# Gate projection of a decoder layer by seven block products

## The chip, the cores and the metric

The kernel runs on one NeuronCore of a Trainium2 chip, in one launch. The metric is the device time of that launch in microseconds (us); lower is better. The engines are TensorE (PE, matrix products), VectorE (DVE), ScalarE (ACT), GpSimd (POOL) and SyncE (SP, which here only issues DMAs). Each engine has its own queue of instructions.

## The reference

One decoder layer on 512 tokens of 1024 channels, all in float32: a mixer (pooling and block-sparse attention), a gated MLP with a causal convolution, and at the end an embedding that is gated by a projection of x. The change concerns the last line.

```python
y = jnp.concatenate([y_pool, y_attn], axis=-1) @ w_out[i]
x = x + rms_norm(y, g_mix_post[i])
h = rms_norm(x, g_ffn_pre[i])
x = x + rms_norm(conv_ffn(h, w_up[i], conv_w[i], conv_b[i], w_down[i]), g_ffn_post[i])
x = x + (p[i] @ w_ple[i]) * jax.nn.sigmoid(x @ w_ple_gate[i])
```

Here x is (512, 1024), `w_ple_gate` (1024, 1024), p (512, 256) and `w_ple` (256, 1024). The MLP has 2816 hidden channels.

## The kernel before

All products keep float32 accuracy by a split: each operand is written as a high and a low part in a reduced format, and three matmuls (low x high, high x low, high x high) are summed in PSUM. `mm3` (lines 190 to 194) issues the three, `split` (lines 196 to 198) makes the parts: ACT copies the high part, DVE subtracts it from the source.

Weights go through the class `_Weights`. Chunks of 1 MB are loaded by SP into one of 2 `raw` buffers and split into pairs (`wh`, `wl`), 6 of which can exist. `take` hands out the next pair; `ahead(n)` issues the splits for n pairs beyond those taken, and with the last split of a chunk the load of the chunk two further on. Nothing reorders this: the order of the Python calls is the order on each engine.

The stages: input projection, attention and pooling (to about 150 us of the profile's clock), output projection and second norm (to about 205), up projection (`project`, 44 column blocks of 24 matmuls; convolution and GELU in `gate_post`, `gelu`, `value_post`), the down projection, and the end. The down projection computes its 2x2 block product with seven products in place of eight (`GROUPS`). Four of these need differences of weight blocks: during the up stage POOL loads rows of `w_down`, forms them in `weight_sums` (line 679) and writes them to the DRAM tile `tsum`, from where they are loaded and split like other weights.

The end starts at about 540 us. `embedding` computes p @ w_ple for four token tiles (48 matmuls, eight outputs). `third_norm` finishes the norm of the MLP and adds the residual x; for tiles 2 and 3 this lies between the embeddings. `put_transposed` transposes x on PE (eight 128x128 blocks a tile) and splits the result into `xT`. `gate_part` is the gate projection: for each column half and token tile a sum over 8 blocks of 128 channels, 24 matmuls. The last output is done in two parts of 256 columns. `gate_out` (lines 789 to 795) finishes an output: sigmoid on ACT, multiplication by the embedding and addition of x on DVE, store on SP. Splits of gate weights stand between the outputs, by `W.ahead((0, 1, 2, 4)[t])`.

Of the kernel before, what the change touches and what calls it, by code (L numbers as in the profile page):

```python
# [24 lines left out]
P = 128  # L25
S = 512
# [34 lines left out]

class _Weights:
# [22 lines left out]

    def load(self, between=None):
        c = self.loaded
        srcs, axis = self.chunks[c]
        raw = self.pool.tile([P, 2048], F32, tag="raw", name=f"raw{c}", bufs=self.RAW)
        if axis == 0:  # L90
            self.raw[c] = raw.rearrange("p (s a b) -> p s a b", s=2, a=2)
            for s, src in enumerate(srcs):
                self.nc.sync.dma_start(self.raw[c][:, s, :src.shape[1], :], src)
        else:
            src = srcs[0]
            self.raw[c] = raw.rearrange("p (a b) -> p a b", a=src.shape[1])
            n = 2 if c < 2 else 1
            step = src.shape[1] // n
            for i in range(n):
                part = slice(i * step, (i + 1) * step)  # L100
                self.nc.sync.dma_start(self.raw[c][:, part, :], src[:, part, :])
                if between is not None:
                    between(i)
        self.loaded += 1

    def ahead(self, n):

        while self.split < min(self.used + n, 2 * len(self.chunks)):
# [3 lines left out]
            raw, (srcs, axis) = self.raw[c], self.chunks[c]  # L112
            if axis == 0:
                view = raw[:, s, :srcs[s].shape[1], :]
            else:
                half = raw.shape[axis] // 2
                part = slice(s * half, (s + 1) * half)
                view = raw[:, part, :] if axis == 1 else raw[:, :, part]
# [5 lines left out]
            self.nc.scalar.copy(pair[0], view)  # L124
            self.nc.vector.tensor_sub(pair[1], view, pair[0].bitcast(F32))  # L125
            self.pairs[self.split] = pair
            self.split += 1
            if s == 1:
                del self.raw[c]
                while self.loaded < min(c + 1 + self.RAW, len(self.chunks)):  # L130
                    self.load()
# [8 lines left out]
def hybrid_layer(ctx, tc, x, p, rel_bias, g_mix_pre, g_mix_post, g_ffn_pre, g_ffn_post, w_in, w_pool,  # L140
# [45 lines left out]
    for n in range(2):  # L186
        for k0 in (0, 4):
            W.rows(w_ple_gate, k0, 4, 512 * n, 512)
# [445 lines left out]
    def value_post(f, pv):  # L634
        dve.scalar_tensor_tensor(M[:, f, :], c_.pop(f), 0.5, pv, op0=ALU.mult, op1=ALU.mult)
        if f >= NK:
            token_sums(f)
# [4 lines left out]
    M = lp.tile([P, NF, S], F32, name="M")  # L642
# [3 lines left out]
    def tokens01(f, n=1):  # L646
        return M[:, f:f + n, :2 * P]

    def tokens23(f, n=1):
        return M[:, f:f + n, 2 * P:]  # L650
# [10 lines left out]
    tw = tw_ctx.enter_context(tc.tile_pool(name="tw", bufs=2, reuse_waits="tile"))  # L661
# [3 lines left out]
    def weight_load():  # L665
        k = len(b_)
        if k < NK:
            b = tw.tile([P, 4, 512], F32, tag="b", name=f"b{k}")
            for i, row in enumerate((k, NK + k)):
                src = w_down[row * P:(row + 1) * P, :].rearrange("p (n c) -> p n c", n=2)  # L670
# [3 lines left out]
    def weight_sums(k):  # L674

        weight_load()
        b = b_[k]
        for o, i0, i1 in ((1, 1, 0), (3, 3, 1), (0, 3, 0), (2, 2, 3)):
            pool.tensor_tensor(out=b[:, o, :], in0=b[:, i0, :], in1=b[:, i1, :], op=ALU.subtract)  # L679
        pool.dma_start(tsum[:, k, :, :], b)  # L680
# [30 lines left out]
    for fb in range(1, NF // 2):  # L711
        for post in (gate_post, value_post):
            for f in (2 * fb, 2 * fb + 1):
# [3 lines left out]
                if u % 2 == 0 and u // 2 < NK:  # L717
                    weight_sums(u // 2)
                u += 1
                if u == 36:  # L720
# [30 lines left out]
    for g, (i, ks) in enumerate(GROUPS):  # L751
# [7 lines left out]
        if ks[-1] == NK - 1:  # L759
            for a in range(2):  # L760
# [7 lines left out]
                elif i == 6:  # L768
# [4 lines left out]
                    if a:  # L773
                        todo = steps([third_norm(t, M[:, 2 * t:2 * t + 2, :]) for t in range(2)])
# [11 lines left out]
    E = M[:, :2 * NT, :].rearrange("p (t n) q -> p t (n q)", n=2)  # L786
    turn = iter(range(2 * NT, 18))

    def gate_out(t, c0, width, ps):
        cols = slice(c0, c0 + width)  # L790
        sg = M[:, next(turn), :width]
        act.activation(sg, ps, AF.Sigmoid)
# [6 lines left out]
    tags = iter(("mm", "mm", "s") * 4)  # L799
# [8 lines left out]
    def gate_part(t, n, c, width):  # L808
        ps = bank(f"g{t}_{n}_{c}")
        sub = [[q[:, :, c:c + width] for q in w] for w in wq]  # L810
        token_product(ps[:, c:c + width], t, sub, range(KD), True, True, h_stationary)
        gate_out(t, n * 512 + c, width, ps[:, c:c + width])

    todo = third_norm(2, M[:, 18:20, :])
    for t in range(NT):
        for n in range(2):
            embedding(t, n)
            next(todo, None)
        if t < 2:
            put_transposed(t, X[t], "pt" if t else "s")  # L820
        if t == 1:
            W.ahead(2)
            todo = third_norm(3, M[:, 20:22, :])
    put_transposed(2, X[2], "pt")
    wq = [W.take() for _ in range(4)]
    for t in range(NT):
        gate_part(t, 0, 0, 512)
        if t == 0:
            put_transposed(3, X[3], "s")
        W.ahead((0, 1, 2, 4)[t])  # L830
    wq = [W.take() for _ in range(4)]
    for t in range(NT - 1):
        gate_part(t, 1, 0, 512)
    for c in range(0, 512, 256):
        gate_part(NT - 1, 1, c, 256)
# [41 lines left out]
```

## Time and profile before

| what | us |
|---|---|
| median of 3 runs (lowest, highest) | 606.15 (604.91, 606.17) |
| the profiled execution | 605.64 |
| its span, first to last instruction | 603.7 |
| PE busy in the span | 596.4 |
| DVE, ACT, POOL busy | 388.4, 280.0, 181.8 |

A profile is one execution, on its own clock that starts at the first instruction. Successive matmuls overlap in it: one of 512 columns is shown with 0.39 us, and the next starts 0.23 us after it. What a matmul costs is therefore read from the distance of starts. A "releaser" is the instruction whose end set a waiting one free.

### The profile page before, as it was taken

The numbers are of one execution on the slowest core, as the hardware profiler recorded it, in microseconds if no ns is written. First come the engines' busy times: TensorE is split into PE (matmuls) and PEld (weight loads), VectorE is DVE, ScalarE is ACT, GpSimd is POOL, SyncE is SP. The second block draws the span as 40 slices with busy tenths as digits, with TensorE's granted clock in tenths as the row PEclk, the third lists the DMA queues.
The fourth block names the chain that finished last, engine by engine and source line by source line (L and its number), as shares of the span: only waits on it lengthen the run. The fifth ranks groups of instructions, "written<-read, shape, count | busy, mean of one in ns | idle before, by whom it ended". The sixth has DMA issues, their size and how long they took to land.

```text
span 603.7 us, 7410 instructions
## 1 busy us (share of the span) xinstructions
PE 596.4 (99%) x2832; PEld 495.9 (82%) x2832; DVE 388.4 (64%) x538; ACT 280.0 (46%) x457; POOL 181.8 (30%) x198
## 2 busy tenths in 40 slices
PE   9999999999999999999999999999999999999997
PEld 5888888888888988888888888888888788888876
DVE  4643676877478657655755764654778776788432
ACT  5532665665455433423532433342555666657320
POOL 2300230046324446666555784214310000002000
PEclk9999999999999999999999999999999999999999
DMA  8675203023660686776757734233174677661211
GB/s 290 209 278 192 70 2 114 25 71 106 209 209 0 243 316 215 283 268 231 259 206 286 270 141 140 71 85 124 69 244 157 202 251 248 210 211 63 105 54 52
DMA packets 56491, 102.35 MB, mean 170 GB/s; under 512 B 2963, under 2 KB 32495, under 8 KB 55048
## 3 DMA queue, kind: packets, MB, share of 16 engines
q1 hardware_dynamic: 48344, 67.71, 34.1%
q0 software_dynamic: 8112, 34.17, 14.8%
q8 instruction: 22, 0.36, 0.3%
q14 instruction: 13, 0.11, 0.1%
HBM read 86.12 MB, written 18.37 MB: 173 GB/s over the span
## 4 chain that ended last, share of the span: by engine, by line
PE 94%; DVE 3%; ACT 1%; issue 1%; POOL 0%; DVEq 0%; POOLq 0%
PE gate L192 6%; PE gate L193 6%; PE valu L192 6%; PE valu L193 6%; PE valu L194 6%; PE gate L194 6%; PE d L192 6%; PE d L194 5%; PE d L193 5%; PE g L193 2%; PE g L194 2%; PE y L193 2%; PE y L192 2%; PE y L194 2%; PE g L192 2%; PE tr L233 2%
## 5 line engine op out<-in xcount | busy, mean ns | idle before, releaser
L125 DVE TENSOR_TENSOR wl<-raw,wh 128x1024 fp32r<-128x1024 f32 (+1 forms) x120 | 149.0, 1249 | 25.4 <-ACT wh L124 24.8
L124 ACT CAST wh<-raw 128x1024 fp32r<-128x1024 f32 (+1 forms) x120 | 120.5, 1021 | 25.5 <-DMA raw<-in_w_down 8.8
L679 POOL TENSOR_TENSOR b<-b 128x512 f32<-128x512 f32 x44 | 69.0, 1577 | 11.2 <-DMA b<-in_w_down 9.4
L192 PE MATMUL gate<-hT,wl 128*128 128x512 f32 x160 | 62.3, 389 | 0.0
L193 PE MATMUL gate<-hT,wh 128*128 128x512 f32 x160 | 62.3, 389 | 0.0
L194 PE MATMUL gate<-hT,wh 128*128 128x512 f32 x160 | 62.2, 389 | 0.0
L192 PE MATMUL valu<-hT,wl 128*128 128x512 f32 x160 | 62.2, 389 | 0.0
L193 PE MATMUL valu<-hT,wh 128*128 128x512 f32 x160 | 62.2, 389 | 0.0
L194 PE MATMUL valu<-hT,wh 128*128 128x512 f32 x160 | 62.2, 389 | 0.0
L192 PE MATMUL d<-wh,ml 128*128 128x512 f32 x154 | 60.0, 390 | 0.7 <-DVE ml L198 0.7
L193 PE MATMUL d<-wl,mh 128*128 128x512 f32 x154 | 59.9, 389 | 0.0
L194 PE MATMUL d<-wh,mh 128*128 128x512 f32 x154 | 59.9, 389 | 0.0
L619 ACT ACTIVATE c<-gate,cols 128x512 f32<-128x512 f32 x20 | 15.5, 776 | 81.4 <-PE gate L194 81.4
L620 DVE SCALAR_TENSOR_TENSOR c<-gate,cols,c 128x511 f32<-128x511 f32 x20 | 14.9, 747 | 43.5 <-ACT c L619 43.5
L464 POOL TENSOR_TENSOR u<-u 128x512 f32<-128x512 f32 x10 | 11.6, 1156 | 81.0 <-ACT u L460 80.6
L194 PEld LDWEIGHTS gate<-hT,wh 128*128 128x128 f32 x160 | 30.0, 188 | 6.3
L194 PEld LDWEIGHTS valu<-hT,wh 128*128 128x128 f32 x160 | 30.0, 188 | 6.3
L192 PEld LDWEIGHTS valu<-hT,wl 128*128 128x128 f32 x160 | 30.0, 188 | 6.3
L222 POOL TENSOR_SCALAR rd<-msd 128x1 f32<-128x1 f32 x4 | 3.1, 783 | 106.4 <-ACT M L217 106.4
L192 PEld LDWEIGHTS gate<-hT,wl 128*128 128x128 f32 x160 | 30.0, 188 | 6.2
L193 PEld LDWEIGHTS valu<-hT,wh 128*128 128x128 f32 x160 | 30.0, 188 | 6.1
L193 PEld LDWEIGHTS gate<-hT,wh 128*128 128x128 f32 x160 | 30.0, 188 | 6.1
(205 smaller groups left out, 1309.9 us busy)
## 6 DMA issues: line engine op xcount, KB each, us to landing
raw<-in_w_up SPq DMA_DIRECT2D x22, 1024.0 KB, 5.3
b<-in_w_down POOLq DMA_DIRECT2D x22, 512.0 KB, 5.0
tsum<-b POOLq DMA_DIRECT2D x11, 1024.0 KB, 5.0
raw<-tsum SPq DMA_DIRECT2D x20, 512.0 KB, 5.0
raw<-in_w_down SPq DMA_DIRECT2D x15, 512.0 KB, 5.9
raw<-in_w_in SPq DMA_DIRECT2D x6, 1024.0 KB, 6.7
raw<-in_w_out SPq DMA_DIRECT2D x4, 1024.0 KB, 5.1
raw<-in_w_ple_gate SPq DMA_DIRECT2D x4, 1024.0 KB, 5.3
```

The costliest lines, as they stand in the source:

```text
L124: self.nc.scalar.copy(pair[0], view)
L125: self.nc.vector.tensor_sub(pair[1], view, pair[0].bitcast(F32))
L192: pe.matmul(o, st[1], mv[0], start=first, stop=False, skip_group_check=more)
L193: pe.matmul(o, st[0], mv[1], start=False, stop=False, skip_group_check=more)
L194: pe.matmul(o, st[0], mv[0], start=False, stop=last, skip_group_check=more)
L222: pool.tensor_scalar(r, ms, add, None, op0=ALU.add)
L233: pe.transpose(ps[:, k * P:(k + 1) * P], src[:, (4 * c + k) * P:(4 * c + k + 1) * P], ident)
L464: pool.tensor_tensor(out=nxt[:, 16:], in0=src[:, 16:], in1=src[:, 16 - (1 << lvl):16 + S - (1 << lvl)], op=ALU.add)
L619: act.activation(c0, pg, AF.Identity, bias=cw[:, 3, f:f + 1], scale=cw[:, 2, f:f + 1])
L620: dve.scalar_tensor_tensor(c0[:, 1:], pg[:, :S - 1], cw[:, 1, f:f + 1], c0[:, 1:], op0=ALU.mult, op1=ALU.add)
L679: pool.tensor_tensor(out=b[:, o, :], in0=b[:, i0, :], in1=b[:, i1, :], op=ALU.subtract)
```

## The change

The gate projection, too, is now computed from seven block products. x is cut into token halves (tiles 0, 1 and 2, 3) and channel halves, `w_ple_gate` into four blocks of 512x512. A product is 12 matmuls x 2 token tiles, all of 512 columns. Products 1, 2 and 3 take blocks of the weight as they are; 4, 5, 6 and 7 take differences of blocks.

Those differences are made in the up stage. After the 11 rounds for `w_down`, `weight_sums` runs four more, on `w_ple_gate`; `split_sums`, called one and two up products after the next round's begin, splits a block in ACT and DVE, and SP writes its high and low parts to the DRAM tile `gsum`. The pool `tw` has 3 buffers for loaded rows in place of 2, and one buffer each for the high and low part; it is closed one up product later. At the end the pairs of products 5, 6, 7 and 4 come from `gsum` straight into the `wh` and `wl` buffers, with no split (`pairs_of`).

On the side of x, the first half (tiles 0 and 1) is transposed and split as before, and POOL adds the two parts up again (`unsplit`) to have them in one piece. For the second half one sum is made from PSUM on DVE, the other differences on POOL (`sums`), and each is split before the product that needs it (`split_sum`). Partial results are copied from PSUM (`keep_sum`) and added on DVE (`add_sum`); outputs of 512 columns are finished by `gate_out`, the last one too. The order at the end is: embeddings and transposes of tiles 0 and 1, product 1, the third norms and embeddings of tiles 2 and 3, their transposes, then products 2, 5, 6, 3, 7, 4. `M` is now two tiles; the second one's place is used again for `S24`.

The core of the diff:

```diff
+    def split_sums(k, half):
+
+        part = slice(2 * half, 2 * half + 2)
+        pair = [tw.tile([P, 2, 512], F32R, tag=f"b{c}", name=f"b{c}{k}_{half}", bufs=1) for c in "hl"]
+        split(pair, b_[k][:, part, :])
+        for c in range(2):
+            dst = gsum[part, :, c, k - NK, :].rearrange("b p c -> p b c")
+            sp.dma_start(dst, pair[c].bitcast(F32))
...
-                if u % 2 == 0 and u // 2 < NK:
-                    weight_sums(u // 2)
+                if u < 2 * NK:
+                    if u % 2 == 0:
+                        weight_sums(u // 2)
+                else:
+                    k, step = divmod(u - 2 * NK, 3)
+                    if step and 0 < k <= KG:
+                        split_sums(NK + k - 1, step - 1)
+                    elif step == 0:
+                        weight_sums(NK + k)
...
+    def unsplit(a):
+        for c, raw in enumerate((A11, A12)):
+            hi, lo = (q[:, a, KG * c:KG * (c + 1)].bitcast(F32) for q in hT)
+            pool.tensor_tensor(out=by_tiles(raw[a]), in0=hi, in1=lo, op=ALU.add)
+
+    def second_half(a):
+
+        t = 2 + a
+        ps = x_transposed(t, 0, "s")
+        act.copy(A21[a], ps)
+        ps = x_transposed(t, 1, "s" if a else "pt")
+        split([q[:, t, KG:] for q in hT], by_tiles(ps))
+        dve.tensor_add(A22[a], ps, A21[a])
+
+    def sums():
+
+        for a in range(2):
+            pool.tensor_tensor(out=A21[a], in0=A11[a], in1=A21[a], op=ALU.subtract)
+            pool.tensor_tensor(out=A11[a], in0=A22[a], in1=A11[a], op=ALU.subtract)
+        for a in range(2):
+            pool.tensor_tensor(out=A12[a], in0=A12[a], in1=A11[a], op=ALU.subtract)
+        for a in range(2):
+            split([q[:, 2 + a, :KG] for q in hT], by_tiles(A22[a]))
...
+    def product(i, a):
+        for k in range(KG):
+            mm3(acc[i][a], operand(i, a, k), [q[:, k % 2, :] for q in wq[k // 2]],
+                k == 0 and i in (1, 2, 5), k == KG - 1, i not in (1, 2, 5))
...
+    for t in range(2, NT):
+        for n in range(2):
+            embedding(t, n)
+        keep_sum(1, t - 2)
+    W.ahead(4)
+    for a in range(2):
+        second_half(a)
+    sums()
+    wq = [W.take() for _ in range(2)]
+    W.ahead(4)
+    acc[2] = [bank(f"g2_{a}") for a in range(2)]
+    for a in range(2):
+        product(2, a)
+        add_sum(1, 2, a)
+        split_sum(6, a)
+    for a in range(2):
+        gate_out(a, 0, rows_of(held[1], a), rows_of(held[1], a))
+    wq = [W.take() for _ in range(2)]
+    W.ahead(4)
+    acc[5] = acc[3] = [bank(f"g5_{a}", "s") for a in range(2)]
+    for a in range(2):
+        product(5, a)
+        keep_sum(5, a)
+        split_sum(3, a)
...
+    for a in range(2):
+        product(7, a)
+        add_sum(5, 7, a)
+    wq = [W.take() for _ in range(2)]
+    product(4, 0)
+    for a in range(2):
+        gate_out(2 + a, 1, rows_of(held[5], a), rows_of(held[5], a))
+    gate_out(2, 0, acc[4][0], rows_of(held[4], 0))
+    product(4, 1)
+    gate_out(3, 0, acc[4][1], rows_of(held[4], 1))
```

Where instructions stand now. First ACT, around the last embedding copies (`M<-e`). Before (`xT0` is the high part of the transposes, `wh114` and `wh115` that of the third and fourth pair of gate weights; L792 is the sigmoid):

```order
L806 COPY M_1936<-e2_1_4603 128x512
L806 COPY M_1936<-e3_0_4612 128x512
L806 COPY M_1936<-e3_1_4621 128x512
L197 CAST xT0_4521<-tr2_0_4629 128x512
L197 CAST xT0_4521<-tr2_1_4636 128x512
L124 CAST wh114_4643<-raw57_4478 128x1024
L124 CAST wh115_4647<-raw57_4478 128x1024
L792 ACT_TABLE_LOAD
L792 ACTIVATE M_1936<-g0_0_0_4653 128x512
```

and now, from the row behind the copy of the last embedding `e3_1` on (`g1_1` is the second of product 1's banks, `wh114` and `wh115` product 2's weights, `z2` and `z3` the room for sums of x, `S24` operands of product 6, L853 the sigmoid):

```order
L933 COPY M0_1937<-g1_1_4666 128x512
L143 CAST wh114_4738<-raw57_4556 128x1024
L143 CAST wh115_4742<-raw57_4556 128x1024
L895 COPY z2_3693<-tr2_0_4756 128x512
L225 CAST xT0_4598<-tr2_1_4762 128x512
L895 COPY z3_3694<-tr3_0_4770 128x512
L225 CAST xT0_4598<-tr3_1_4776 128x512
L225 CAST xT0_4598<-z2_3693 128x512
L225 CAST xT0_4598<-z3_3694 128x512
L225 CAST S24_4597<-z0_3691 128x512
L225 CAST S24_4597<-z1_3692 128x512
L853 ACT_TABLE_LOAD
```

The casts of `wh114` and `wh115` stood behind the embedding copies and two transposes' casts; now they stand behind the copies of the last embedding and of a bank of product 1 and ahead of the transposes, and the sigmoid table is loaded after the casts of product 6's operands.

Second DVE, from the casts' low halves on. Before, outputs (L793, L794) alternate with splits:

```order
L125 TENSOR_TENSOR wl114_4644<-raw57_4478,wh114_4643 128x1024
L125 TENSOR_TENSOR wl115_4648<-raw57_4478,wh115_4647 128x1024
L793 TENSOR_TENSOR M_1936<-M_1936 128x512
L794 TENSOR_TENSOR M_1936<-M_1936,S1_1937 128x512
L198 TENSOR_TENSOR xT1_4522<-tr3_0_4682,xT0_4521 128x512
L198 TENSOR_TENSOR xT1_4522<-tr3_1_4689,xT0_4521 128x512
L793 TENSOR_TENSOR M_1936<-M_1936 128x512
L794 TENSOR_TENSOR M_1936<-M_1936,S1_1937 128x512
L125 TENSOR_TENSOR wl116_4726<-raw58_4512,wh116_4725 128x1024
```

and now (`g2_0`, `g2_1` are product 2's banks, `wl120` and `wl121` product 3's weights, the last row product 3's first operand):

```order
L226 TENSOR_TENSOR xT1_4599<-z3_3694,xT0_4598 128x512
L937 TENSOR_TENSOR M0_1937<-M0_1937,g2_0_4802 128x512
L226 TENSOR_TENSOR S24_4597<-z0_3691,S24_4597 128x512
L937 TENSOR_TENSOR M0_1937<-M0_1937,g2_1_4803 128x512
L226 TENSOR_TENSOR S24_4597<-z1_3692,S24_4597 128x512
L854 TENSOR_TENSOR M0_1937<-M0_1937 128x512
L855 TENSOR_TENSOR M0_1937<-M0_1937,S1_1939 128x512
L854 TENSOR_TENSOR M0_1937<-M0_1937 128x512
L855 TENSOR_TENSOR M0_1937<-M0_1937,S1_1939 128x512
L144 TENSOR_TENSOR wl120_4843<-raw60_4754,wh120_4842 128x1024
L144 TENSOR_TENSOR wl121_4847<-raw60_4754,wh121_4846 128x1024
L226 TENSOR_TENSOR S24_4597<-z0_3691,S24_4597 128x512
```

In front of product 3's weights and operand there now stand the splits for product 6 and the two finished outputs.

Third SP, the DMAs of the end. Before:

```order
L101 DMA raw56_4441<-in_w_ple_gate 128x4x512
L101 DMA raw57_4478<-in_w_ple_gate 128x4x512
L101 DMA raw58_4512<-in_w_ple_gate 128x4x512
L101 DMA raw59_4651<-in_w_ple_gate 128x4x512
L795 DMA out<-M_1936 128x512 x7
L795 DMA out<-M_1936 128x256 x2
```

and now (pairs 116 and 117 belong to product 5, 118 and 119 to 6, 122 and 123 to 7, 124 and 125 to 4):

```order
L141 DMA wh118_4794<-gsum_75 128x1024
L141 DMA wl118_4795<-gsum_75 128x1024
L141 DMA wh119_4798<-gsum_75 128x1024
L141 DMA wl119_4799<-gsum_75 128x1024
L856 DMA out<-M0_1937 128x512 x2
L141 DMA wh122_4884<-gsum_75 128x1024
L141 DMA wl122_4885<-gsum_75 128x1024
L141 DMA wh123_4888<-gsum_75 128x1024
L141 DMA wl123_4889<-gsum_75 128x1024
L141 DMA wh124_4926<-gsum_75 128x1024
```

The loads of products 7 and 4 now stand behind the first two stores of outputs.

## Rows read from the trace of the kernel before

**Rows 1.** Page: busy time of each engine, and GB/s in 40 slices.

```profile
PE 596.4 (99%) x2832; PEld 495.9 (82%) x2832; DVE 388.4 (64%) x538; ACT 280.0 (46%) x457; POOL 181.8 (30%) x198
...
GB/s 290 209 278 192 70 2 114 25 71 106 209 209 0 243 316 215 283 268 231 259 206 286 270 141 140 71 85 124 69 244 157 202 251 248 210 211 63 105 54 52
```

**Rows 2.** Timeline, PE at the end: start, duration (us), line, operation.

```profile
589.67 0.39 PE L194 MATMUL g<-wh,xT 128*128 128x512 f32 x1
...
593.07 0.39 PE L194 MATMUL g<-wh,xT 128*128 128x512 f32 x1
593.29 0.28 PE L192 MATMUL g<-wh,xT 128*128 128x256 f32 x1
...
598.93 0.28 PE L194 MATMUL g<-wh,xT 128*128 128x256 f32 x1
```

**Rows 3.** Timeline, PE, two gaps of the gate projection.

```profile
556.09 0.39 PE L192 MATMUL g<-wh,xT 128*128 128x512 f32 x1
556.50 0.50 PE L193 MATMUL g<-wl,xT 128*128 128x512 f32 x1
...
579.06 0.39 PE L192 MATMUL g<-wh,xT 128*128 128x512 f32 x1
579.78 0.50 PE L193 MATMUL g<-wl,xT 128*128 128x512 f32 x1 [0.33 <-DVE wl L125]
```

**Rows 4.** Timeline, DVE: last addition of a 512- and of a 256-column output.

```profile
594.85 0.69 DVE L794 TENSOR_TENSOR M<-M,S 128x512 f32<-128x512 f32 x1
...
600.12 0.43 DVE L794 TENSOR_TENSOR M<-M,S 128x256 f32<-128x256 f32 x1
```

**Rows 5.** DMA issues, stores at 595.6 and 600.6: KB, us to landing.

```profile
out<-M SPq DMA_DIRECT2D x1, 256.0 KB, 2.0
...
out<-M SPq DMA_DIRECT2D x1, 128.0 KB, 1.9
```

**Rows 6.** Timeline, PE: last embedding matmul, first gate matmul.

```profile
552.25 0.39 PE L194 MATMUL e<-wh,pT 128*128 128x512 f32 x1
...
553.28 0.48 PE L192 MATMUL g<-wh,xT 128*128 128x512 f32 x1
```

**Rows 7.** Timeline, ACT, from the last embedding on.

```profile
552.68 0.58 ACT L806 COPY M<-e 128x512 f32<-128x512 f32 x1 [0.78 <-PE e L194]
...
554.12 2.02 ACT L124 CAST wh<-raw 128x1024 fp32r<-128x1024 f32 x2
556.16 1.28 ACT L792 ACT_TABLE_LOAD   x1
559.33 0.60 ACT L792 ACTIVATE M<-g 128x512 f32<-128x512 f32 x1 [1.89 <-PE g L194]
```

**Rows 8.** Timeline, DVE: norm of the last tile, two weight splits.

```profile
552.24 1.28 DVE L738 SCALAR_TENSOR_TENSOR S<-z,rd,S 128x1024 f32<-128x1024 f32 x1 [0.75 <-POOL rd L223]
...
555.22 2.36 DVE L125 TENSOR_TENSOR wl<-raw,wh 128x1024 fp32r<-128x1024 f32 x2
```

**Rows 9.** Groups of DVE, 215 to 353 us: count, busy, mean ns, idle before.

```profile
L125 DVE TENSOR_TENSOR wl<-raw,wh 128x1024 fp32r<-128x1024 f32 x24 | 34.8, 1451 | 4.1 <-ACT wh L124 4.1
L630 DVE SCALAR_TENSOR_TENSOR sq<-sq,c 128x512 f32<-128x512 f32 x14 | 16.3, 1165 | 0.8 <-ACT sq L629 0.8
...
L635 DVE SCALAR_TENSOR_TENSOR M<-c,valu 128x512 f32<-128x512 f32 x12 | 8.2, 682 | 8.8 <-PE valu L194 8.8
```

**Rows 10.** The same, 360 to 428 us.

```profile
L125 DVE TENSOR_TENSOR wl<-raw,wh 128x1024 fp32r<-128x1024 f32 x13 | 15.8, 1217 | 0.0
...
L630 DVE SCALAR_TENSOR_TENSOR sq<-sq,c 128x512 f32<-128x512 f32 x7 | 4.8, 683 | 0.0
```

**Rows 11.** Line 679 on POOL: ns minimum/median/maximum, first and last start.

```profile
L679 POOL TENSOR_TENSOR b<-b x44: 1275/1310/2280, 213.7 to 352.1; 128x512 f32<-128x512 f32 x44
```

**Rows 12.** Windows: busy us (count) PE, PEld, DVE, ACT, POOL, PEclk, DMA share, GB/s.

```profile
208.00:224.00 16.00, 16.00 (x107) 14.69 (x106) 9.65 (x11) 6.33 (x9) 6.02 (x5) 1.00 1.02 379
360.00:400.00 40.00, 40.00 (x178) 33.15 (x177) 21.00 (x26) 13.35 (x17) 12.79 (x13) 1.00 0.33 106
```

More of the change, by code (lines that the diff above doesn't have):

```diff
@@ L185, in hybrid_layer, with gate_sum @@
     W.rows(w_ple, 0, 2, 0, D)
-    for n in range(2):
-        for k0 in (0, 4):
-            W.rows(w_ple_gate, k0, 4, 512 * n, 512)
+    gsum = dram.tile([4, P, 2, KG, 512], F32, name="gsum")
+    def gate_sum(i):
+        place = {7: 0, 5: 1, 4: 2, 6: 3}[i]
+        return [[gsum[place, :, c, k0:k0 + 2, :] for c in range(2)] for k0 in (0, 2)]
+    for i in GATE:
+        if i in (1, 2, 3):
+            row, n = {1: (0, 0), 2: (KG, 0), 3: (KG, 1)}[i]
+            W.rows(w_ple_gate, row, KG, 512 * n, 512)
+        else:
+            W.pairs_of(*gate_sum(i))
     def mm3(o, st, mv, first, last, more=False):
@@ L666, in weight_load @@
         k = len(b_)
[L667 to L670, printed above, removed]
+        if k < NK + KG:
+            w, k, half = (w_down, k, NK) if k < NK else (w_ple_gate, k - NK, KG)
+            b = tw.tile([P, 4, 512], F32, tag="b", name=f"b{len(b_)}")
+            for i, row in enumerate((k, half + k)):
+                src = w[row * P:(row + 1) * P, :].rearrange("p (n c) -> p n c", n=2)
                 pool.dma_start(b[:, 2 * i:2 * i + 2, :], src)
@@ L773, in hybrid_layer @@
                     if a:
[L774 removed]
+                        todo = steps([third_norm(t, M(2 * t, 2)) for t in range(2)])
         W.ahead(4)
@@ L816, in hybrid_layer @@
         for n in range(2):
             embedding(t, n)
[L818 to L835, printed above, removed]
+        first_half(t)
+    next(thirds[0])
+    wq = [W.take() for _ in range(2)]
+    acc[1] = acc[6] = acc[7] = acc[4] = [bank(f"g1_{a}", "pt") for a in range(2)]
+    for a in range(2):
+        product(1, a)
+    next(thirds[1])
+    for _ in steps(thirds):
+        pass
+    for a in range(2):
+        unsplit(a)
+    for t in range(2, NT):
+        for n in range(2):
+            embedding(t, n)
+        keep_sum(1, t - 2)
@@ new lines, in hybrid_layer @@
+    wq = [W.take() for _ in range(2)]
+    W.ahead(4)
+    for a in range(2):
+        product(6, a)
+        keep_sum(6, a)
+        split_sum(7, a)
+    wq = [W.take() for _ in range(2)]
+    W.ahead(4)
+    for a in range(2):
+        product(3, a)
+        gate_out(a, 1, add_sum(6, 3, a), rows_of(held[6], a))
+    wq = [W.take() for _ in range(2)]
+    W.ahead(4)
+    for a in range(2):
+        product(7, a)
+        add_sum(5, 7, a)
+    wq = [W.take() for _ in range(2)]
+    product(4, 0)
```

114 lines of the change are left out of this document (82 added, 32 removed).

## The prediction

> **What bounds the kernel now.** First I read busy shares and the chain that ended last: TensorE (PE) is busy for 596.4 of 603.7 us [rows 1], so a matmul less is time less, as long as nothing takes its place. Then the PE timeline of the gate projection. Its 512-column matmuls start 0.2267 us apart (15 between 589.67 and 593.07), the 256-column ones at the end 0.12 us apart (47 between 593.29 and 598.93) [rows 2]. At two places the gap is longer, 0.41 us at 556.50 and 0.72 us at 579.78, the second waiting for a weight split on VectorE (DVE); with the slow restart of 0.34 us after each, some 0.9 us is lost [rows 3]. Then the end: from the start of the last matmul to the end of the last add 1.62 us with 256 columns, and 2.47 us for an earlier output with 512 [rows 2, 4]; the stores land 1.9 and 2.0 us after issue [rows 5].
>
> **What goes.** Before, the gate projection is 4 row tiles x 2 column halves x 8 blocks x 3 terms, 168 matmuls of 512 columns and 48 of 256 (the last output is cut in two). Now it is 7 products x 2 tiles x 4 blocks x 3 terms, 168 of 512. What goes is the 48 x 0.12 = 5.76 us. The two waits of 0.9 us go too, since the splits behind which PE waited stand elsewhere. Embeddings (48 matmuls) and 32 transposes stay.
>
> **What comes late instead.** I follow the new order on the old clock; up to 540 us nothing in this part moves. Product 1 (24 matmuls, 5.44 us) is put ahead of the embeddings of tiles 2 and 3, so that their last matmul starts at 552.25 + 5.44 = 557.69 [rows 6]. Sixteen transposes later (eight took 0.8 us between 552.25 + 0.23 and 553.28 [rows 6]; I allow 0.85) PE is ready for product 2 at 559.6. Its weights are cast only now: ScalarE (ACT) has to copy the last embedding (0.43 us after its last matmul started, as at 552.68) and the held product first, each a step of 0.5 us, so the cast runs from 559.1 to 560.15 [rows 6, 7]. DVE's half takes 1.22 us [rows 10], to 561.4 at best. PE's second matmul was due at 559.85: 1.55 us lost.
>
> It is rather more, for GpSimd now works in this stretch. Rows show what that does to DVE. While GpSimd (POOL) forms the weight sums of the down projection, a DVE operation with both inputs in SBUF takes 1451 ns (128x1024) or 1165 ns (128x512), one with an input in PSUM 682 ns [rows 9]; with POOL mostly idle the first two take 1217 and 683 ns [rows 10]. So an operation with two SBUF inputs and a POOL operation exclude each other. POOL's own 128x512 subtraction takes 1310 ns in the median and up to 2280, one DVE operation more [rows 11]. The four additions that rebuild the transposes stand behind the norms of tiles 2 and 3: their mean squares come on ACT at 547.9 and 549.0 by the same stepping, then DVE's two operations per tile (the longer 1.28 [rows 8]) alternate with POOL's small ones until 554.2. The first addition (1.31), DVE's last norm operation (1.28) and three more additions take it to 560.7; the weight split starts then and ends at 562.0. I take 2.1 us lost.
>
> The Trainium skill has this as a lock (SBUF — State Buffer, Terms): GpSimd and VectorE arbitrate for one shared port pair, held for the whole instruction, and the loser blocks fully. The rows agree for two SBUF inputs and not for a PSUM input. Read literally it makes a rival, below.
>
> Products 2, 5 and 6 then run without a gap, to 567.2, 572.65 and 578.1. Product 3 is the next that I see late. Behind the second weight split (563.1) DVE splits one transposed half and adds the next, 0.6 each, to 564.3; POOL's differences start there. The fourth is product 6's second operand, and three DVE splits with SBUF inputs get in between: 564.3 + 4 x 1.31 + 3 x 0.68 = 571.6. ACT casts it (0.62), loads the sigmoid table (1.28) and makes the first sigmoid (0.60) [rows 7], to 574.0. DVE meanwhile waits for POOL's fifth difference, splits (to 573.5), and waits for the sixth, to 574.85. Then stand in DVE's queue, in this order, four multiplies and adds of the first two outputs (2.7 us), the two weight splits of product 3 (2.36 us) [rows 8] and its operand's low half (0.6): 580.45. PE was ready at 578.1: 2.35 us lost. Behind it products 3, 7 and 4 follow without a gap: product 7's operands are split by 582.3, and PE comes to them at 585.9.
>
> Of the table load the Trainium skill says (ScalarE: Activation LUTs, What ACT_TABLE_LOAD costs) that a drain of about 1.38 us comes on top of 1.28 us. In this trace ACT waits for PE after the load until 559.33 [rows 7], so no run here shows it. By it the end would be some 0.6 us later, 604.8 (an estimate from that page).
>
> **The end.** The last output now has 512 columns: 2.47 - 1.62 = +0.85 us, its store +0.1 us; and the last matmul starts 0.2267 instead of 0.12 us before PE's end, -0.11.
>
> **Cost nothing, and why.** Sixteen more POOL subtractions (21 us and more) and eight more splits (10 to 12 us of DVE, 8 of ACT) fall between 342 and 420 us. There POOL, DVE and ACT are busy 12.8, 21.0 and 13.4 of 40 us [rows 12], and an up product has four others, 21.8 us, before its PSUM bank is used again. SP gets 16 stores of 512 KB that wait for those splits, ahead of the loads of w_up and w_down; these are issued two chunks, four products, ahead, so a few us late is early enough. DMA is at 106 GB/s there; 12.6 MB more is about 33 us at the 379 GB/s that it holds for 16 us elsewhere [rows 12], in some 75. The single buffer of each half makes the second split wait for the first store to land; a store of 256 KB lands 2.0 us after issue [rows 5], one of 512 KB by that rate some 0.7 us later, and the splits are 5.44 us apart. If that cover failed, a product would wait for what is missing, 1 to 4 us. Below nothing: I see no edit before 540 us that takes work off PE. Tiles 2 and 3 are normed under product 1 and the embeddings (11 us) and are done at 556.8, two us ahead of their transposes. A stall of 2 us is longer than any the trace has; that PE keeps its full clock through it (granted 1.00, the 2.4 GHz level) [rows 12] is assumed.
>
> **Sum.** -5.76 - 0.9 + 2.1 + 2.35 + 0.85 + 0.1 - 0.11 = -1.4 us against the profiled execution of 605.64 us (span 603.7 and 1.9 around it): 604.2. The timed runs of before have their median 0.5 us higher, at 606.15, so against them the gain may read 1.9 us, and 0.2% (about what a measurement of this kernel can tell from no change) is 1.2 us.
>
> **Rivals.**
> A, the forecast, spreads by the time of a POOL operation. At 1.24 us the end comes 0.7 us earlier, at 1.4 us 0.9 us later, because some ten of them stand in the two chains: 603.0 to 605.6.
> B, the collisions don't happen, because the operations meet at other moments or DVE goes first each time. Then product 2 waits 1.45 us, product 3 not at all (its operand is ready at 576.9, PE at 577.4): -1.4 - 0.65 - 2.35 = -4.4, 601.2. For it: POOL has some 2 us of slack before product 6's second operand is wanted. Against: rows 9, and that here POOL and DVE have six and five such operations in the same 11 us.
> C, the literal lock: PSUM-reading operations wait too. Then the two additions and the high-half splits also queue behind POOL, product 3 waits 4.2 us, and the end is 2.4 us later than in A: 606.6. Against it speaks the 682 ns.
> D, the slower side: the split sums come late from DRAM. SP issues the loads of products 7 and 4 (4.2 MB) behind two stores that wait for DVE's add at 577.5. The last pair is needed at 592.7, so 4.7 MB has 592.7 - 577.5 - 2.0 = 13.2 us: from 357 GB/s down it decides, at 323 the gain is gone, at 300 and less it is slower by over 0.2%. For: at the kernel's start, when loads queue, the first slice has 290 GB/s [rows 1]; that gives 16.3 us, 3.1 late: 607.3. Against: 379 GB/s over 16 us from 208 us on [rows 12]. The loads of products 5 and 6 have the same rate to keep, but what is lost there comes off product 3's wait.
> That fewer matmuls are not run is excluded: the new program has 168.
>
> **Chances.** A 0.50, B 0.20, C 0.08, D 0.15, and 0.07 for a wait in the up stage or a slower clock (605 to 609). Faster by over 0.2%: 0.32 of A, all of B: 0.52. Same: 0.16 of A, 0.06 of C, 0.04 of D, 0.03 of the rest: 0.29. Slower: 0.19. The range runs from B to D, 601.0 to 607.3; A alone has 603.0 to 605.6.
>
> **What would show it.** PE with 2784 instead of 2832 matmuls at 0.2267 us; in its waits two new ones of about 2 us, both for DVE: the second matmul of product 2 for a weight split, the first of product 3 for an operand's low half. DVE operations of twice their time at 560 to 575 us, POOL's likewise. No PE wait for a DMA of the split sums, and none before 540 us. The prediction is wrong if these waits are absent (then B), if PE waits for DMA in products 7 or 4 (D), or if the time is lost in the up stage.

## The result, and the profile after

The changed kernel takes 601.99 us (median of 4 runs, 601.81 to 602.6) against 605.56 us before (4 runs, 604.91 to 606.17): a ratio of 0.9943, 95% interval 0.9926 to 0.996. Two later sets of five runs gave 0.9952 (0.994 to 0.9965) and 0.9946 (0.9934 to 0.9958). By these ratios the gain is 2.9 to 3.5 us, where 1.4 (against the profiled execution of before; 1.9 against the median as it stood) was forecast.

The page of the profiled execution (601.81 us, span 600.0), busy time of each engine and GB/s in 40 slices, as in [rows 1]:

```profile
PE 589.7 (98%) x2784; PEld 488.8 (81%) x2784; DVE 425.9 (71%) x556; ACT 292.9 (49%) x476; POOL 231.3 (39%) x232
...
GB/s 293 205 270 207 70 2 118 22 72 106 210 209 2 227 361 236 365 324 365 323 182 117 234 211 211 279 211 276 144 243 160 146 296 200 269 211 63 288 202 220
```

PE has 2784 matmuls, 48 fewer. DVE, ACT and POOL carry 37.5, 12.9 and 49.5 us more, and the last three slices, 105, 54 and 52 GB/s before, have 288, 202 and 220. PE's waits (total, times, longest, us):

```profile
PE idle L314 <- POOL ident masks.py:199: 1.4, 1, 1.4
PE g L220 <- DVE S L226: 0.9, 1, 0.9
PE g L221 <- DVE wl L144: 0.8, 1, 0.8
PE d L220 <- DVE ml L226: 0.7, 1, 0.7
PE pt L451 <- DVE L L436: 0.5, 1, 0.5
PE tr L261 <- DVE hT L226: 0.4, 1, 0.4
PE g L220 <- ACT wh L143: 0.4, 1, 0.4
```

The two new waits of the gate projection (g) stand second (product 3) and third (product 2); a wait for the weight cast, at product 2's first matmul, adds 0.4. On PE's timeline (start, duration, line, in brackets the wait before it):

```profile
557.20 1.91 PE L873 MATMUL tr<-ident,S 128*128 128x128 f32 x16
559.47 0.50 PE L220 MATMUL g<-wh,xT 128*128 128x512 f32 x1 [0.36 <-ACT wh L143]
560.73 0.50 PE L221 MATMUL g<-wl,xT 128*128 128x512 f32 x1 [0.76 <-DVE wl L144]
...
576.77 0.39 PE L222 MATMUL g<-wh,S 128*128 128x512 f32 x1
578.07 0.50 PE L220 MATMUL g<-wh,S 128*128 128x512 f32 x1 [0.91 <-DVE S L226]
...
585.00 0.39 PE L220 MATMUL g<-wh,s7l 128*128 128x512 f32 x1
585.41 0.50 PE L221 MATMUL g<-wl,s7h 128*128 128x512 f32 x1
```

These are the two instructions of the prediction: product 2's second matmul and product 3's first. Against an even step of 0.2267 us and with the slow restarts, 1.57 us are lost at the first place and 1.2 at the second. The small gap at 585.41, in product 7, costs 0.3 us with its restart and is not in the two later profiles of this kernel. Its matmul waited for a load: the low half of product 7's second pair left at 577.53 and landed 7.8 us later.

**A part that is not the change.** 0.7 us of the difference of the spans (603.7 - 600.0) arose before the gate projection. The first matmul of the value projection started at 11.03 us and took 0.50, in the profile of before at 12.15 and took 0.80:

```profile
11.03 0.50 PE L220 MATMUL v<-wh,hT 128*128 128x512 f32 x1
11.37 0.40 PE L221 MATMUL v<-wl,hT 128*128 128x512 f32 x1
11.61 0.40 PE L222 MATMUL v<-wh,hT 128*128 128x512 f32 x1
```

Of the fourteen profiles of this study six have it at 11.0 to 11.6 us and the first transpose of the embedding stage at 541.78 to 541.85 us; eight have it at 12.15 or 12.16 and the transpose at 542.54 to 543.75. No line of that early part differs between the kernels, and kernels with and without an edit fell on both sides.

What goes with it is TensorE's clock at the start. In the profile of before the matmuls of the value projection (v) first follow each other every 0.43 us, the step that e3 below has at a granted clock of 0.50 (the 1.2 GHz level), and later every 0.23 us; in the changed kernel's (above) it is 0.34 and then 0.24 us from the first. The chain of before that ended last (start, us) shows both:

```profile
12.95 0.43 PE v L193
13.38 0.43 PE v L194
...
15.95 0.23 PE v L192
```

The trace's first record of the granted clock, 1.00, begins at 15.35 us there and at 9.74 in the changed kernel's profile (earlier there is no record, and the views print 1.00). Over the fourteen it begins at 9.74 to 10.96 us in the six and at 15.35 to 17.94 in the eight, and among the eight a later start always has a later transpose. Before (15.35, transpose at 542.54) stands in line with the next kernels, all with the change in them (15.64 and 542.64, 15.78 and 542.75). So the difference ahead of the gate projection goes with the start of the clock, and the change shows no cost there. What starts the clock sooner or later is not shown.

So profiles are compared from that first transpose (T) on, in the table in us; the median and its ratio to before are of timed runs.

| kernel | median | ratio, 95% interval | T | T to start of last matmul | T to end of span |
|---|---|---|---|---|---|
| before | 605.56 | | 542.54 | 56.39 | 61.16 |
| changed | 601.99 | 0.9943 (0.9926-0.996) | 541.80 | 52.82 | 58.20 |
| c1, changed again | 602.35 | 0.9952 (0.994-0.9965) | 541.85 | 52.53 | 57.95 |
| c2, changed again | 602.3 | 0.9946 (0.9934-0.9958) | 541.78 | 52.50 | 57.92 |
| e1 early casts | 600.77 | 0.9928 (0.9916-0.9941) | 542.64 | 50.85 | 56.26 |
| e2 late outputs | 606.0 | 1.0022 (1.0012-1.0031) | 541.83 | 56.88 | 62.27 |
| e3 rebuild twice | 604.44 | 0.998 (0.9971-0.9989) | 542.75 | 54.99 | 60.45 |
| e4 split tail | 602.98 | 0.9961 (0.9949-0.9973) | 541.84 | 53.47 | 58.36 |
| e5 loads first | 601.35 | 0.9936 (0.9919-0.9952) | 543.75 | 52.76 | 58.15 |
| e6 three together | 600.0 | 0.991 (0.9898-0.9923) | 542.88 | 50.56 | 55.42 |
| e7 one more | 603.04 | 0.9962 (0.9949-0.9975) | 543.00 | 53.56 | 59.00 |
| e8 loads, then outputs | 601.12 | 0.993 (0.9918-0.9942) | 542.96 | 50.94 | 56.34 |
| e9 halves apart | 600.72 | 0.9918 (0.9906-0.9931) | 542.76 | 51.20 | 56.14 |
| e10 outputs only | 601.69 | 0.9943 (0.9928-0.9957) | 541.80 | 52.68 | 58.10 |

From T on the change gains 3.0 to 3.2 us, as the timed ratios say.

### The profile page after: what moved, and what is told of

Its sections match the earlier page's. It is cut to its first block, busy times and chain, and to the rows that moved or that the text cites. A ratio compares the mean times of both kernels' runs of the same rounds, so it can differ in the third digit from the quotient of the medians.

```text
span 600.0 us, 7466 instructions
## 1 busy us (share of the span) xinstructions
PE 589.7 (98%) x2784; PEld 488.8 (81%) x2784; DVE 425.9 (71%) x556; ACT 292.9 (49%) x476; POOL 231.3 (39%) x232
## 3 DMA queue, kind: packets, MB, share of 16 engines
q0 software_dynamic: 9264, 38.36, 17.4%
## 4 chain that ended last, share of the span: by engine, by line
PE 90%; DVE 4%; ACT 3%; POOL 1%; issue 1%; POOLq 0%; DVEq 0%; ACTq 0%
PE gate L221 6%; PE valu L221 6%; PE gate L220 6%; PE valu L220 6%; PE gate L222 6%; PE valu L222 6%; PE d L220 6%; PE d L221 6%; PE d L222 6%; PE y L222 2%; PE y L221 2%; PE y L220 2%; PE o L471 1%; DVE wl L144 1%; PE up L220 1%; PE up L222 1%
## 5 line engine op out<-in xcount | busy, mean ns | idle before, releaser
L144 DVE TENSOR_TENSOR wl<-raw,wh 128x1024 fp32r<-128x1024 f32 (+1 forms) x118 | 158.1, 1347 | 30.6 <-ACT wh L143 30.2
L143 ACT CAST wh<-raw 128x1024 fp32r<-128x1024 f32 (+1 forms) x118 | 118.8, 1022 | 28.6 <-DMA raw<-in_w_up 11.9
L715 POOL TENSOR_TENSOR b<-b 128x512 f32<-128x512 f32 x60 | 95.8, 1606 | 12.1 <-DMA b<-in_w_down 9.6
L492 POOL TENSOR_TENSOR u<-u 128x512 f32<-128x512 f32 x10 | 11.6, 1156 | 79.9 <-ACT u L488 79.5
L659 ACT ACTIVATE sq<-sq 128x512 f32<-128x512 f32 x22 | 13.9, 632 | 53.2 <-DVE sq L658 53.2
L647 ACT ACTIVATE c<-gate,cols 128x512 f32<-128x512 f32 x20 | 15.4, 772 | 49.1 <-PE gate L222 49.1
```

Source lines behind the costliest of these rows:

```text
L492: pool.tensor_tensor(out=nxt[:, 16:], in0=src[:, 16:], in1=src[:, 16 - (1 << lvl):16 + S - (1 << lvl)], op=ALU.add)
L647: act.activation(c0, pg, AF.Identity, bias=cw[:, 3, f:f + 1], scale=cw[:, 2, f:f + 1])
L659: act.activation(sq, sq, AF.Tanh, scale=GELU_A * GELU_C)
```

## The experiments

All start from the changed kernel. Three sets were run, each beside the kernel before: c1, e1, e2, e3; then e4 to e7; then c2, e10, e8, e9.

**c1 and c2**, no edit.

> The changed kernel once more, as the standard for the runs beside it. Both theories: 3 to 4 us under the kernel before (601.99 against 605.56 in the medians so far). Of the profiled difference of 3.7 us, 0.7 was there before the gate projection began (its first embedding transposes 0.7 us earlier, no line of that part changed). If that part is scatter between executions, the transposes of this run start at another time again, 0.2 us or more from 541.8, and the gate projection from there to its last matmul takes the same time as in the first profile within 0.1 us.

> The changed kernel once more, beside the next three. In nine profiles so far, whatever the gate projection did, the first matmul of the value projection (v) started either between 11.0 and 11.6 us or at 12.15, and the embedding transposes at 541.8 or at 542.5 and later. Expected of this run: one of the two, and from the first embedding transpose to the start of the last matmul 52.5 to 52.8 us, as in the two profiles of this kernel; 0.995 of the kernel before.

Measured: c1 missed on both counts. T was 541.85, where another start was expected, and the stretch from T to the last matmul was 52.53 us, 0.29 less than in the first profile: the gap at 585.41 is missing. c2 is as expected (541.78, 52.50). These two alone do not show the scatter; the profiles of the other kernels do.

**e1**, the cast of product 2's weights ahead of the embeddings of tiles 2 and 3:

```
     for _ in steps(thirds):
         pass
+    W.ahead(2)
     for a in range(2):
         unsplit(a)
```

> Product 2's weights are cast and split before the embeddings of tiles 2 and 3. Theory 1 (the queue of ScalarE): its second matmul waited because the cast stood behind the last embedding's copy; both waits there (0.36 and 0.76 us, with the restart 1.57 us late) go, and since the work in front of product 3 moves up too, nothing of it comes back: 1.6 us less than the changed kernel, up to 2.0. Theory 2 (one chain, GpSimd's differences at its end): product 3's operand comes when it came, and the 1.6 us is waited there instead, 0.9 + 1.6 us before its first matmul: no change in time.

Measured: 1.7 us less from T on, ratio 0.9928 against 0.9952. Both waits of product 2 are gone, and of the gate projection this alone is left:

```profile
PE g L220 <- DVE S L226: 0.8, 1, 0.8
```

Product 3's wait did not grow (0.78 us). Theory 1: ScalarE's queue order was the cause, and the cost did not come back. The splits now do meet GpSimd's additions and take 4.6 us in place of 2.36, in turns with them, but early enough that PE does not wait.

**e3**, two more additions of GpSimd, and **e7**, one more:

```
-    for a in range(2):
+    for a in (0, 0, 1):          # e3; e7: unsplit(0, (0,)) ahead of the old loop
         unsplit(a)
```

> GpSimd rebuilds tile 0's transposes a second time (two additions more, 3 us, same result), so that its additions reach to about 562 us and lie beside the two weight splits of product 2, as the prediction had it. Theory 1 (an operation of VectorE with two inputs in SBUF and one of GpSimd exclude each other; in the changed kernel they missed each other by 0.3 us): the first weight split takes twice its 1.2 us or more, and product 2's second matmul comes 1.0 us later: 1.0 us more than the changed kernel (0.6 to 1.6). Rival (they run side by side, each a little slower): 0 to 0.2 us more.

> One more addition of GpSimd (one half of tile 0 is rebuilt twice, same result) instead of the two more of e3_rebuild_twice. The first weight split of product 2 meets one running addition, and product 2's second matmul comes 1.0 us later than in the changed kernel, a stall of about 1.8 us beside the 0.36 before it: nearly the 2.1 that was predicted. Theory 1 (a stall of this length leaves the clock alone): 1.0 us more than the changed kernel. Theory 2 (PE's granted clock falls to half behind it, as behind the 2.84 us of e3_rebuild_twice, where 8 matmuls started 0.43 instead of 0.23 us apart): 2.6 us more.

Measured in e3: 2.5 us more from T on. VectorE's two weight splits take 4.43 us in place of 2.36, and the second starts at 563.65:

```profile
560.43 4.43 DVE L144 TENSOR_TENSOR wl<-raw,wh 128x1024 fp32r<-128x1024 f32 x2 [3.98 <-ACT wh L143]
```

GpSimd's last two additions, in the view of line 889 for 561 to 563 us (durations minimum/median/maximum in ns, first and last start):

```profile
L889 POOL TENSOR_TENSOR z<-xT,xT x2: 1297/1304/1311, 560.1 to 561.3; 128x512 f32<-128x512 f32 x2
```

The split could have gone first at 561.3, when the addition begun at 560.1 ended. GpSimd's next one went, undelayed, and the split had its turn at 562.6. So the two exclude each other here, and the expectation missed: VectorE waited for two additions, not one. The wait at product 2's second matmul is 2.84 us, 2.08 more. The rest is the clock. Windows of PE (busy, count, granted clock, DMA share, GB/s) in e3, and then in e7:

```profile
562.00:564.00 2.00, 0.22 (x1) 1.00 1.05 412
564.00:566.00 2.00, 2.00 (x8) 0.83 1.02 407
566.00:568.00 2.00, 2.00 (x6) 0.50 0.69 277
568.00:570.00 2.00, 2.00 (x8) 0.82 0.05 18
570.00:572.00 2.00, 2.00 (x10) 1.00 0.00 0
```

```profile
561.00:563.00 2.00, 0.43 (x2) 0.89 1.03 390
563.00:565.00 2.00, 2.00 (x5) 0.50 1.03 417
565.00:567.00 2.00, 2.00 (x8) 0.76 0.95 379
567.00:569.00 2.00, 2.00 (x11) 1.00 0.32 127
```

Behind the stall the granted clock falls to 0.50, the 1.2 GHz level; in e3 nine steps from 565.27 us on take 3.64 us instead of 2.04, 1.6 us lost. In e7 the wait is 1.57 us (behind the 0.36 for the cast) and the clock falls as well. e7 took 1.0 us more from T on, the number of its theory 1, but by theory 2's way: product 2's second matmul 0.8 later, the half clock 1.4, and product 3's wait, 1.2 with its restart, gone, because PE came later to an operand that had moved less. Its total alone would have misled.

**e2**, the first two outputs behind the splits of product 3, **e5**, behind product 7's loads as well, and **e10**, behind product 4's too:

```
     for a in range(2):
         product(2, a)
...
-    for a in range(2):
-        gate_out(a, 0, rows_of(held[1], a), rows_of(held[1], a))
...
     for a in range(2):
         product(5, a)
         keep_sum(5, a)
         split_sum(3, a)
+    (the two lines)              # e2
     wq = [W.take() for _ in range(2)]
     W.ahead(4)
+    (the two lines)              # e5; e10: behind the next W.ahead(4), below product 6
```

> The first two outputs (table load, two sigmoids, four multiplies and adds) are put behind the splits of product 3's operand instead of ahead of them. Theory 1 (queues of ScalarE and VectorE): the casts of product 3's weights follow at 570.2, its low half is there at about 574.5 instead of 578.0, and the wait of 0.91 us with its slow restart goes: 1.2 us less than the changed kernel. Theory 2 (GpSimd's differences): the last two difference operations end at 572.5, and what they allow is no earlier than now; the wait stays, 0 to 0.2 us less.

> As e2_late_outputs, but the first two outputs are called behind the issue of product 7's loads, so that on SyncE these four loads stand ahead of the two stores that wait for VectorE; ScalarE and VectorE keep the order of e2_late_outputs. Theory 1 (in e2_late_outputs the wait for product 3's operand went, and what was paid instead came from the place of the loads in SyncE's queue): the loads go out near 572 instead of 579.7, no wait at product 7, and the 1.2 us of product 3 are gained: 1.2 us less than the changed kernel. Theory 2 (DMA itself is too slow for the split sums): product 4's loads, still behind the stores, come late in their turn, PE waits for them near 587 us, and the time is 0 to 3 us above the changed kernel.

> As e5_loads_first, but the first two outputs are called behind the issue of product 4's loads too, so that no load of a split sum stands behind a store that waits. Theory 1 (queue order): product 3's wait of 0.91 us and its restart go, and neither product 7 nor product 4 waits for a DMA (in e5_loads_first product 4's second matmul did, 1.1 us): 1.2 us less than the changed kernel, and 51.4 us from the first embedding transpose to the last matmul. Theory 2 (DMA too slow for the split sums): the wait at product 4 stays, 0 to 0.4 us less.

Measured: the wait for product 3's operand is gone in all three, so the outputs in VectorE's and ScalarE's queues made it. But each time another came. In e2 product 7 waits for its weights, 4.3 us more from T on; PE, then SyncE's queue:

```profile
584.71 0.47 PE L220 MATMUL g<-wh,s7l 128*128 128x512 f32 x1 [2.06 <-DMA wh<-gsum]
586.44 0.52 PE L221 MATMUL g<-wl,s7h 128*128 128x512 f32 x1 [1.26 <-DMA wl<-gsum]
```

```profile
577.65 1.66 SPq L856 DMA_DIRECT2D out<-M  x2
579.74 0.33 SPq L141 DMA_DIRECT2D wh<-gsum  x1
```

The two stores wait for VectorE until 577.65, and product 7's loads behind them leave at 579.74; in the changed kernel at 575.97. The clock fell to half here too. In e5 the loads go first (572.34), and product 4's, still behind the stores, are late in the profiled execution, the slowest of its six runs (600.21 to 603.71 us):

```profile
592.71 0.50 PE L221 MATMUL g<-wl,xT 128*128 128x512 f32 x1 [1.14 <-DMA wl<-gsum]
```

From T on e5 is 0.2 us above c1; 1.9 us more lie ahead of T (543.75), with the latest start of the clock. Its median is 1.0 us below c1's, its lowest run 1.4. That lowest run has a span of 598.4 us, which leaves 56.6 from the earliest T seen (541.78), 1.3 less than c1: the 1.2 us of product 3 and no wait at product 4. So the load seems to come in time in some runs and not in others; only the late one was profiled. In e10 no load waits, but 2.7 us of outputs on VectorE push the additions of products 3 and 7 back, and product 4 cannot write its bank before the last of these has read it:

```profile
589.13 0.50 PE L220 MATMUL g<-wh,xT 128*128 128x512 f32 x1 [1.07 <-DVE M L937]
```

No gain (0.2 us more from T on). Theory 1 was right on the cause, and its gain did not come in e2 and e10. The wait for a load, theory 2 of e5, is real in e2 and e5; that it goes when the loads stand ahead of the stores (product 7's in e5, product 4's in e10) shows that the order of SyncE's queue makes it possible.

**e4**, the last output in two halves of one PSUM bank (`gate_out` gets the column bounds as arguments), and **e9**, with e10's and e1's edits, the last but one in halves and the last one's matmuls between them:

```
-    product(4, 1)
-    gate_out(3, 0, acc[4][1], rows_of(held[4], 1))
+    for q0 in (0, 256):
+        for k in range(KG):
+            mm3(acc[4][1][:, q0:q0 + 256], operand(4, 1, k), [q[:, k % 2, q0:q0 + 256] for q in wq[k // 2]],
+                False, k == KG - 1, True)
+        gate_out(3, 0, acc[4][1], rows_of(held[4], 1), q0, q0 + 256)
```

and in e9, on top of e8:

```
-    product(4, 0)
+    half_product(0)              # columns 0 to 255 of product(4, 0)
...
-    gate_out(2, 0, acc[4][0], rows_of(held[4], 0))
+    gate_out(2, 0, acc[4][0], rows_of(held[4], 0), 0, 256)
     product(4, 1)
     gate_out(3, 0, acc[4][1], rows_of(held[4], 1))
+    half_product(256)
+    gate_out(2, 0, acc[4][0], rows_of(held[4], 0), 256, 512)
```

> The last output is formed in two halves of 256 columns, as the kernel before did. Theory: 12 matmuls of 512 columns (12 x 0.2267 = 2.72 us) become 24 of 256 (24 x 0.12 = 2.88), +0.16 us; behind the last one stand operations of half the size, 1.62 instead of 2.47 us, and the store lands 0.1 earlier: 0.7 to 0.8 us less than the changed kernel. Rival (the last store's landing sets the end and does not depend on the size of the operations before it): 0 to 0.2 us less.

> e8_loads_then_outputs, with the last but one output cut into two halves of 256 columns, the second of which PE forms last, behind the other output's 12 matmuls. In e4_split_tail the second half waited 0.5 us for ScalarE's reading of the first half in the same bank, and came 0.93 us later instead of 0.16. If that reading was the cost, 12 matmuls between the halves take it away: +0.16 - 0.85, some 0.5 to 0.7 us less than e8_loads_then_outputs. Rival (VectorE is still busy with the whole output before when the half comes, and halves gain nothing): 0 to 0.2 us less.

Measured: e4 gains nothing, 0.4 us more from T on. From the start of the last matmul to the end of the last addition it has 1.62 us, as before, but the second half waited for ScalarE to read the first:

```profile
593.89 0.39 PE L220 MATMUL g<-wh,xT 128*128 128x256 f32 x1 [0.47 <-ACT M L854]
```

Its last matmul came 0.93 us later, not 0.16. The kernel before, which e4 was to copy, forms its two halves in two banks (`gate_part` calls `bank` for each), and there the second half does not wait [rows 2]. With the halves apart (e9) that wait is gone, and the last addition ends 0.48 us earlier from T than in e8; the span 0.2, and the intervals (0.9906 to 0.9931, 0.9918 to 0.9942) overlap. Whether it pays is open.

**e6**, e1 + e4 + e5, and **e8**, e1 + e10:

> The edits of e1_early_casts, e4_split_tail and e5_loads_first together. If the three costs are independent: -1.6 - 1.1 - 0.7 = 3.4 us less than the changed kernel, about 599.0, and from the first embedding transpose on PE waits for nothing. If they share one chain, so that taking one wait brings another out (as in e2_late_outputs): no more than 2.4 us less than the changed kernel, with a new wait named in the trace.

> e10_outputs_only and e1_early_casts together, the last output whole. Independent costs: -1.2 - 1.7 = 2.9 us less than the changed kernel, 49.7 us from the first embedding transpose to the last matmul, no wait of PE in the gate projection. Rival (a wait comes back at another place, as in e2_late_outputs): under 2 us less.

Measured: e6 2.5 us less from T on, ratio 0.991 (0.9898 to 0.9923), the lowest here (e9's interval overlaps it) and faster than both kernels; none of the waits of products 2, 3, 7 and 4 is left but e4's 0.47. The parts add up with the sizes measured, not with those expected: e1's -1.7, product 3's -1.2, e4's +0.4. From T its loads of product 4 left 1.8 us earlier than e5's, PE came to them about as much earlier, and they were in time: the last one landed 8.5 us after its issue, where e5's took 10.0. What makes that differ is not shown. e8 gains 1.6, all of it e1's: e10's wait of 1.07 us stands in it. e6 without e4's halves should be 0.4 us faster; it was not run.

## Why the prediction was right or wrong

- **What goes, -5.76 and -0.9 us: right.** 48 matmuls are gone, and no DVE wait stands where the two old ones were.
- **Product 2, +2.1: the place right, the size 1.57.** The cast runs behind the last embedding's copy and the held product, as said, and the split behind it. The failed step is the collision. From T, GpSimd's four additions were to end after 18.2 us and ended after 17.4, at 559.15 (they started 0.4 us earlier than said and took 6.08 us, not 6.5); VectorE's split began 0.3 us later, and nothing collided. Timeline of POOL, then of DVE:

```profile
553.07 6.08 POOL L889 TENSOR_TENSOR z<-xT,xT 128x512 f32<-128x512 f32 x4
```

```profile
559.45 2.36 DVE L144 TENSOR_TENSOR wl<-raw,wh 128x1024 fp32r<-128x1024 f32 x2 [3.99 <-ACT wh L143]
...
564.12 2.59 DVE L226 TENSOR_TENSOR xT<-z,xT 128x512 fp32r<-128x512 f32 x2
566.64 0.68 DVE L937 TENSOR_TENSOR M<-M,g 128x512 f32<-128x512 f32 x1
...
572.20 0.88 DVE L854 TENSOR_TENSOR M<-M 128x512 f32<-128x512 f32 x1 [0.83 <-ACT M L853]
...
578.53 1.29 DVE L226 TENSOR_TENSOR s7l<-z,s7h 128x512 fp32r<-128x512 f32 x2
```

  The prediction's 1.55 without it comes close partly by luck: the second matmul started 1.39 us behind its turn, and 0.18 is the slow restart, which the prediction left out. Where the two do meet, VectorE waited through one addition (e7) or two (e3), and the clock's fall came on top.
- **Product 3, +2.35: the place and the queue right, the size 1.2.** From T, GpSimd's first difference was to start after 21.8 us and started after 21.4; the fourth was to end after 29.1 and ended after 27.8. The failed step is the 4 x 1.31 + 3 x 0.68: GpSimd's differences took 1.29 to 1.74 us, 6.4 together and not 7.3, while VectorE's two splits with SBUF inputs took 2.59 us in place of the 1.29 that two take beside an idle GpSimd (564.12 and 578.53 above). The two do not pay alike: over these four differences VectorE lost 1.8 us in three splits, GpSimd 1.1. A second step failed with it: the first multiply of the outputs was put behind GpSimd's sixth difference, 3.25 us after the fourth; it started 2.63 us after it (572.20 above), beside the end of the sixth, and took 0.88 us in place of 0.69. So the operand came 1.64 us earlier than said and PE 0.36: 1.07 us, and 0.13 by the restart.

```profile
563.18 1.29 POOL L903 TENSOR_TENSOR z<-z,z 128x512 f32<-128x512 f32 x1 [4.03 <-DVE z L898]
564.55 1.62 POOL L904 TENSOR_TENSOR z<-z,z 128x512 f32<-128x512 f32 x1
566.13 1.74 POOL L903 TENSOR_TENSOR z<-z,z 128x512 f32<-128x512 f32 x1
567.95 1.62 POOL L904 TENSOR_TENSOR z<-z,z 128x512 f32<-128x512 f32 x1
```

  That an operation with an input in PSUM is not held up is right: 0.68 us at 566.64 (above), inside GpSimd's difference of 566.13 to 567.87, as [rows 9] had it. The Trainium skill (SBUF — State Buffer, Terms) has the loser of the shared port pair block fully for the whole instruction; e3, whose split sat through two additions, agrees for two SBUF inputs. Rival C, the prediction's wider reading by which PSUM-reading operations wait too, did not happen.
- **The table load: 1.28 us and nothing on top.**

```profile
570.24 1.28 ACT L853 ACT_TABLE_LOAD   x1
571.54 1.16 ACT L853 ACTIVATE M<-M 128x512 f32<-128x512 f32 x2
```

  The load starts 0.01 us behind the cast in front of it, and the first sigmoid 0.02 us behind the load. The Trainium skill's further drain of 1.38 us (ScalarE: Activation LUTs, What ACT_TABLE_LOAD costs) is not in this trace, and the 604.8 us by that page did not come.
- **The end, +0.95 us: 0.65.** From the start of the last matmul to the end of the last addition 2.47 us, as said (594.62 to 597.09). From the last matmul to the end of the span it was 4.77 us and is 5.38 to 5.42. The failed term is the store's +0.1: from the end of the last addition to the end of the span it was 3.16 us and is 2.95. Why is not shown.
- **Cost nothing: right in the up stage.** PE is busy for all of 215 to 420 us (columns as in [rows 12]), beside 144 us of POOL, and T comes no later than the start of the clock explains (above):

```profile
215.00:420.00 205.00, 205.00 (x910) 169.91 (x908) 149.41 (x142) 81.17 (x104) 144.32 (x123) 1.00 0.75 262
```

- **Rival D, DMA late: 0.3 us in the first profile of the changed kernel, none in the two later ones.** Its own sign, PE waiting for a DMA in product 7, was there: from 580 us on the DMA engines are full until product 4 runs, and the gap of 0.18 us at 585.41 is a wait for product 7's second pair. A delay of 3.8 us of those loads (e2) made it the largest wait of the program.

```profile
580.00:583.00 3.00, 3.00 (x15) 2.47 (x14) 1.18 (x2) 0.63 (x1) 0.00 (x0) 1.00 0.98 322
583.00:586.00 3.00, 2.98 (x14) 2.16 (x13) 2.23 (x5) 0.63 (x1) 0.00 (x0) 1.00 1.02 418
586.00:589.00 3.00, 3.00 (x15) 2.47 (x14) 1.34 (x2) 0.63 (x1) 0.00 (x0) 1.00 1.03 414
```

- **The clock through a stall of 2 us: assumed, and not so.** It holds 1.00 behind 0.76 us (c1) and 1.14 us (e5), and falls with 1.57 (e7). That the length alone decides is not shown. Had the predicted 2.1 us come, some 1.4 us of half clock might have come with it (an estimate from e7), a term that the sum does not have.

So the time lies between the forecast (-1.4) and rival B (-4.4): product 2 went as in B, product 3 lost half of what A said. It is no rival's time: 601.99 us is 1.0 below A's 603.0 to 605.6 (whose ends are 0.5 us wider than the 0.7 and 0.9 us worked out for them), 0.8 above B's 601.2, and inside the stated range only because that reaches down to B. The misses are 0.5, 1.15 and 0.3 us in the same direction, 1.95 less than the sum, -3.35. From T, c1 and c2 have -3.2, and the first profile -3.0; its gap at 585.41 is the 0.3 between them. The last 0.1 is not placed.

## What to carry to other kernels

A wait that comes from the order of an in-order queue goes when the order changes, but what is moved waits somewhere else: write out every queue it passes, the DMA queue too, and ask who is next behind it (e2, e5 and e10 each found another). Move the step whose result nobody else is waiting for early (a weight cast), before the step that frees nothing late (an output). And before a difference of a microsecond is explained, see whether TensorE's clock started alike in both profiles, and compare them from a point behind that start, having looked whether the change costs anything ahead of it.

## What was not expected of the hardware

- TensorE's granted clock fell to 0.50 (1.2 GHz) around three stalls and stayed there for some 3.4 us each: 1.57 us (e7, just before PE went on), 2.84 us (e3, 1.5 us after it went on) and 2.06 + 1.26 us (e2, 0.3 us after). e3 lost 1.6 us by it. Behind 1.14 us (e5) it held 1.00.
- In e3 a VectorE operation with two SBUF inputs lost two turns in a row to GpSimd (560.1 and 561.3, 1.30 us each, undelayed); in e1 the two alternated. What decides is not shown.
- A matmul into one half of a PSUM bank waited 0.47 us for ScalarE's reading of the other half (e4, e6); with the halves in two banks (before) it did not. Whether the chip or the order set by semaphores asks for it, the runs do not tell.
- TensorE's clock came up at 9.7 to 11.0 us or at 15.4 to 17.9 us of the profile, behind the same lines of the kernel, and the last stage then began 0.7 to 2.0 us later. What decides was not tried.
